# Last stage's addition of x by accumulating DMA for most tiles; sums of weights moved behind evictions or lower parts; first norm's row loaded first

## The chip, the cores and the metric

One core of a Trainium2 chip. The metric is device time in microseconds (us) of one execution of the program, as a median of several runs. The engines of the core are TensorE (PE; its weight loads are listed as PEld), VectorE (DVE), ScalarE (ACT), GpSimd (POOL) and SyncE (SP). SP issues nearly all DMAs of this kernel, each engine takes its instructions in order, and the engines wait for each other and for DMAs by semaphores.

## What is computed

One decoder layer over 1024 tokens of width 1024, in float32:

```python
def swiglu(h, w_gate, w_up, w_down):
    return (jax.nn.silu(h @ w_gate) * (h @ w_up)) @ w_down          # D_FF = 2816

x = x + 0.5 * swiglu(rms_norm(x, ffn1_norm), ffn1_w_gate, ffn1_w_up, ffn1_w_down)
h = rms_norm(x, mix_norm)
fq, fk, fv, f_logit, sq, sk, sv, g_fox, g_sb = split_columns(h @ w_in)
...                                   # forgetting attention y_fox, stick-breaking attention y_sb
merged = (jax.nn.sigmoid(g_fox) * (y_fox @ w_branch_fox) + jax.nn.sigmoid(g_sb) * (y_sb @ w_branch_sb))
x = x + merged @ w_out
x = x + 0.5 * swiglu(rms_norm(x, ffn2_norm), ffn2_w_gate, ffn2_w_up, ffn2_w_down)
x = x + jax.nn.sigmoid(rms_norm(x, ple_norm) @ w_ple_gate) * (p @ w_ple_proj)
```

## The kernel before

**Products.** Every large product is done block by block with seven products in the place of eight (Strassen's scheme in Winograd's form): a block of 256 columns of a weight is a 2x2 grid of 512 x 128 blocks, x is a 2x2 grid of 512 x 512 blocks, and seven products of sums and differences of these are added up in PSUM banks. In the code `(n, m)` is product m of weight block n: m = 1, 6, 7, 4 use one bank one after the other ("b"), 5 and 3 another ("d"), 2 a third ("a"). Each operand is split into a high part, rounded to the type TensorE multiplies at full rate (`float32r`), and a low part, the rest: ScalarE casts the high part (L105 for weights, L645 for x), VectorE subtracts for the low part (L106, L649). A product takes twelve matmuls of 512 columns: high by high, high by low, low by high, four each (L613 in `product`; L513 for the products with the down weights).

**Stages.** First FFN up and gate (22 weight blocks), first FFN down, mix projection (6 blocks of gates in this manner, the rest plainly), attention, output projection, second FFN up and gate, its down part, and the last stage, 4 blocks of `w_ple_gate`. The last chunk of a down part makes the next stage's norm and operands step by step (`up_begin`, `up_step`, `up_first`). All of these but attention are recorded in the order in which they are to stand: no scheduler moves an instruction, so the order on each engine is the order of the code.

**Steps of an up part.** `up_order` lists the products. At step s the loop takes one product, evicts what it finished (`evict`), then calls `begin(s)`, which makes the operands that only the later products need, and then `prep` for the product four steps ahead, which casts and subtracts its weight operand. The first steps of a stage (s = 0, 1, ...) are (2,1), (1,5), (2,2), (1,6), (1,7), (2,6), (2,5), (1,3), (2,7), (1,4). In `begin`, `sums(2)` (L576 to L578) makes the two sums of weight block 2 that (2,6) and (2,7) need, in a new tile and in place; `combo_s(q, 7)` casts and subtracts the four pieces of x's operand for m = 7; `last_sum` (L581) makes the weight operand of m = 2; `combo_d` (L727 and L728 in the first FFN, where x comes in rows, `rows()`; L730 elsewhere, where it comes transposed) and `combo_e` make x's operand for m = 4. Before the steps stand `combo_u` (a difference, L709 and L710, then the cast L645 on ScalarE) and `combo_s(j, 6)` (the low part L649, which waits for that cast).

**evict.** m = 1 and 6: ScalarE copies bank "b" (L770, L772; L1305 and L1307 in the mix projection, L1718 and L1720 in the last stage). The next product of that bank starts behind the copy. m = 7: a copy, and VectorE adds bank "d"; m = 3, which goes on in "d", starts behind that.

**Down parts.** `make_down` does the same with chunks of the hidden width. Step (c, i) is product i of chunk c, four banks by turns (t = 0..3), each evicted by an addition to x on VectorE (L521; L519 in the output projection). `prep` for the next step comes first, and for i = 0, 1 (behind the first chunk), 3 and 4 it ends with `wd_sums`, two subtractions of 128x1024 (L446), which are used by a `prep` one to three steps later.

**Start.** `first_entry`: ScalarE's queue issues three loads of gains (L161), then the row of the first norm (L1523, tile `PT`); SP issues x's rows and the weights. `spread` multiplies the row by ones to bring it to all partitions (L241) and copies it to SBUF (L243); `rows_mul` (L270) multiplies x's rows by it and by the rows' factors (`rt`). In the traces `in_ffn_norm_dram` stands for the first norm's row as well as for the gain of the second FFN's norm.

**Last stage.** `ple_start`: the result of a weight block is a pair of tiles of 128 x 1024, E[n][0] and E[n][1]. `fetch(n, i)` loads the matching tiles of the projection of p (`pd`, "p_proj") and of x (`xe`, "x_end"), which had been stored; `finish(n, i)` multiplies the sigmoid by the first (L1705), adds the second (L1706) and stores (L1707). The table `AT` says behind which step each is called. All these DMAs are on SP's queue, and a store waits there for VectorE. POOL has one operation in these steps, `last_sum` of block 3.

Of the kernel before, what the change touches and what calls it, by code (L numbers as in the profile page):

```python
# [18 lines left out]
P = 128  # L19
# [17 lines left out]
def tile_hybrid_decoder_layer(  # L37
# [122 lines left out]
    for i, gain in enumerate((mix_norm, ffn2_norm, ple_norm)):  # L160
        nc.scalar.dma_start(gains[:, i, :], gain[0])  # L161
# [260 lines left out]
    def make_down(wdown, hid, chunks, scale, sum_tags):  # L422
# [60 lines left out]
        def prep(c, i):  # L483
# [12 lines left out]
            if c and i < 2 or i in (3, 4):  # L496
                wd_sums(c, (1, 2, None, 3, 4)[i])
# [25 lines left out]
        return types.SimpleNamespace(wd_block=wd_block, wd_sums=wd_sums, load_hid=load_hid, operand=operand, prep=prep, product=product, chunks=chunks)  # L523
# [9 lines left out]
    def make_up(N, src, nm_, tags, first_fn, first_done=None, over=None):  # L533
# [204 lines left out]
        def begin(s):  # L738

            if s == 0:  # L740
                sums(2, nc.vector)
                for q in range(4):
                    combo_s(q, 7)
            elif s == 2:
                last_sum(1, nc.vector)
                last_sum(2, nc.vector)
            if 0 < s < 3:
                combo_d(2 * s - 2)
                combo_d(2 * s - 1)
            if 2 < s < 7:  # L750
                combo_e(s - 3)
        return types.SimpleNamespace(a=combo_a, b=combo_b, t=combo_t, l=combo_l, u=combo_u, s=combo_s, load=load, prep=prep, sums=sums, last_sum=last_sum, plain=plain, silu=silu, product=product, begin=begin, E=E, B=B, bank_of=bank_of)

    def ffn(N, wg, wu, wd, resid, hid, tags, entry, tail):
# [50 lines left out]
        with tc.manual_schedule():  # L805
# [30 lines left out]
            for s, (c, i) in enumerate(steps):  # L836
# [676 lines left out]
    def first_entry(F):  # L1513
# [20 lines left out]
        F.load(1)  # L1534
        for t in range(4):
# [60 lines left out]
        for j in range(2, 4):  # L1596
            F.u(j)
            F.s(j, 6)
# [59 lines left out]
    def second_entry(F):  # L1658
# [9 lines left out]
        for i in range(7):  # L1668
# [15 lines left out]
            for t in range(4):  # L1684
                matmuls(t)
                evict(t)
                up_step(N, Xm, xm, F, i, t)
        up_first(N, F)

    def ple_start():  # L1690
# [5 lines left out]
        def fetch(n, i, tag):  # L1696
            r = T[n, i] = [slot(tag, [P, 2, 512]) for _ in range(2)]
# [3 lines left out]
        def finish(n, i, h=slice(0, 2), cols=slice(0, 512)):  # L1701

            pt, xt = T[n, i]
            e = E[n][i]
            nc.vector.tensor_mul(e[:, h, cols], e[:, h, cols], pt[:, h, cols])  # L1705
            nc.vector.tensor_add(e[:, h, cols], e[:, h, cols], xt[:, h, cols])  # L1706
            nc.sync.dma_start(out[0, (2 * n + i) * P:(2 * n + i + 1) * P, :].rearrange("p (h n) -> p h n", h=2)[:, h, cols], e[:, h, cols])  # L1707
# [28 lines left out]
        AT = {4: [(fetch, 0, 1, "Q")], 5: [(finish, 0, 0)], 6: [(fetch, 1, 0, "KH"), (fetch, 1, 1, "T")], 7: [(finish, 0, 1)], 8: [(fetch, 2, 1, "Q")],  # L1736
# [60 lines left out]
```

## Time and profile before

| | |
|---|---|
| median of 3 runs | 2258.29 us (2256.14 to 2258.59) |
| the profiled execution | 2258.84 us |
| its span | 2257.1 us |
| instructions | 30539 |
| granted TensorE clock, mean over the span | 0.998 |
| DMA | 298.04 MB, 132 GB/s over the span |

A row of the timeline is: start (us from the span's start), duration of the run of equal instructions, engine, line, operation, output<-inputs, shape, count, and in brackets the idle time of the engine just before and what ended it. A q behind an engine's name is its queue: the issue of a DMA. A row of the table by stretches is: window, its length, then busy time and number of instructions of PE, PEld, DVE, ACT and POOL, the granted clock, the busy share of the DMA engines and GB/s. A row of waits is: who waited, for whom, us in total, times, longest. A row of DMA issues is: output<-input, count, size, median us from issue to landing. The names are those of the tiles' tags (X, H, T, Q, KH, KL, GF, RN, PT, WH, WL, RAW, Y), which many tiles share.

### The profile page before, as it was taken

The numbers are of one execution on the slowest core, as the hardware profiler recorded it, in microseconds if no ns is written. First come the engines' busy times: TensorE is split into PE (matmuls) and PEld (weight loads), VectorE is DVE, ScalarE is ACT, GpSimd is POOL, SyncE is SP. The second block draws the span as 40 slices with busy tenths as digits, with TensorE's granted clock in tenths as the row PEclk, the third lists the DMA queues.
The fourth block names the chain that finished last, engine by engine and source line by source line (L and its number), as shares of the span: only waits on it lengthen the run. The fifth ranks groups of instructions, "written<-read, shape, count | busy, mean of one in ns | idle before, by whom it ended". The sixth has DMA issues, their size and how long they took to land.

```text
span 2257.1 us, 30539 instructions
## 1 busy us (share of the span) xinstructions
PE 2218.3 (98%) x11210; PEld 1881.7 (83%) x11210; DVE 1518.7 (67%) x2371; ACT 1005.1 (45%) x1805; POOL 808.2 (36%) x782
## 2 busy tenths in 40 slices
PE   8999999999999999999999999999999999999998
PEld 6788888888888898999898888888888888888886
DVE  7755555598888334666678885889555554778797
ACT  6433333333355435555566663245333333434453
POOL 1344444210011336556566663520544353200110
PEclk9999999999999999999999999999999999999999
DMA  4232323394332434333323466741423232655325
GB/s 141 84 123 83 118 92 110 138 336 151 124 117 85 141 91 140 89 99 85 89 53 94 117 201 208 259 149 57 140 80 130 80 131 80 240 208 192 120 95 214
DMA packets 196183, 298.04 MB, mean 132 GB/s; under 512 B 28729, under 2 KB 108857, under 8 KB 196034
## 3 DMA queue, kind: packets, MB, share of 16 engines
q1 hardware_dynamic: 195600, 296.08, 39.6%
q8 instruction: 88, 1.44, 0.3%
q14 instruction: 61, 0.50, 0.1%
q10 hardware_dynamic: 434, 0.02, 0.0%
HBM read 196.14 MB, written 83.13 MB: 124 GB/s over the span
## 4 chain that ended last, share of the span: by engine, by line
PE 87%; DVE 8%; ACT 2%; issue 2%; DMA 1%; POOL 0%; SPq 0%; DVEq 0%; ACTq 0%; POOLq 0%
PE ps L613 39%; PE ps L513 20%; PE ps L885 7%; PE ps L893 5%; PE ps L1488 4%; PE ps L1226 3%; PE ps L561 3%; PE ps L1200 2%; PE ps L1142 1%; PE ps L1141 1%; PE ps L1047 1%; DVE PT L1208 1%; DVE H L106 1%; DVE RN L1104 1%; DVE GF L1104 1%
## 5 line engine op out<-in xcount | busy, mean ns | idle before, releaser
L513 PE MATMUL ps<-H,H 128*128 128x512 f32 x2184 | 498.0, 389 | 1.9 <-DVE X L521 1.2
L513 PEld LDWEIGHTS ps<-H,H 128*128 128x128 f32 x2184 | 409.2, 188 | 87.8 <-issue 3.0
L613 PE MATMUL ps<-H,WL 128*128 128x512 f32 x1164 | 276.6, 390 | 3.7 <-DVE WL L106 2.0
L613 PEld LDWEIGHTS ps<-H,WL 128*128 128x128 f32 x1164 | 218.2, 188 | 50.6 <-DVE WL L106 2.4
L187 POOL TENSOR_TENSOR PT<-PT,PT 128x512 f32<-128x512 f32 x27 | 34.9, 1294 | 405.6 <-ACT PT L184 404.7
L613 PE MATMUL ps<-H,Q 128*128 128x512 f32 x624 | 148.4, 389 | 0.0
L521 DVE SCALAR_TENSOR_TENSOR X<-ps,X 128x512 f32<-128x512 f32 x168 | 108.6, 687 | 49.3 <-PE ps L513 49.3
L613 PE MATMUL ps<-X,WL 128*128 128x512 f32 (+1 forms) x588 | 138.9, 385 | 2.1 <-ACT Y L772 1.6
L613 PEld LDWEIGHTS ps<-H,Q 128*128 128x128 f32 x624 | 117.1, 188 | 24.3
L613 PE MATMUL ps<-H,PT 128*128 128x512 f32 x540 | 131.7, 396 | 3.2 <-ACT GF L1720 3.2
L613 PEld LDWEIGHTS ps<-X,WL 128*128 128x128 f32 x588 | 108.8, 188 | 24.7 <-ACT Y L772 2.0
L613 PEld LDWEIGHTS ps<-H,PT 128*128 128x128 f32 x540 | 103.2, 192 | 25.4 <-ACT GF L1720 3.6
L139 POOL TENSOR_TENSOR WL<-RAW,WH 128x512 fp32r<-128x512 f32 (+1 forms) x84 | 97.5, 1182 | 67.2 <-ACT WH L129 43.5
L1208 DVE TENSOR_TENSOR PT<-ps,PT 128x512 fp32r<-128x512 f32 (+1 forms) x160 | 100.0, 627 | 30.0 <-ACT PT L1202 29.2
L885 PE MATMUL ps<-WH,H 128*128 128x256 f32 x768 | 116.1, 287 | 0.8 <-ACT RN L950 0.8
L893 PE MATMUL ps<-H,WH 128*128 128x512 f32 x384 | 115.1, 406 | 0.0
L1226 PE MATMUL ps<-PT,X 128*128 128x256 f32 (+1 forms) x640 | 102.4, 286 | 6.2 <-DVE PT L1208 5.2
L1202 ACT CAST PT<-ps 128x512 fp32r<-128x512 f32 (+1 forms) x160 | 87.1, 549 | 42.7 <-PE ps L1200 41.6
L1226 PEld LDWEIGHTS ps<-PT,X 128*128 128x128 f32 x640 | 90.2, 190 | 16.6 <-DVE PT L1208 10.1
L885 PEld LDWEIGHTS ps<-WH,H 128*128 128x128 f32 x768 | 101.4, 190 | 2.7 <-ACT RN L950 1.3
L414 POOL TENSOR_TENSOR PT<-GF,RN 128x512 f32<-128x512 f32 x20 | 33.7, 1685 | 188.7 <-DVE GF L795 188.7
L1154 POOL TENSOR_TENSOR T<-T,l 128x128 f32<-128x128 f32 (+3 forms) x64 | 73.2, 1147 | 71.9 <-DVE l L1153 69.7
(435 smaller groups left out, 4777.7 us busy)
## 6 DMA issues: line engine op xcount, KB each, us to landing
hidden<-PT SPq DMA_DIRECT2D x40, 512.0 KB, 3.1
WH<-in_ffn_w_gate_dram SPq DMA_DIRECT2D x38, 512.0 KB, 4.9
Q<-hidden SPq DMA_DIRECT2D x24, 512.0 KB, 6.2
hidden<-RN SPq DMA_DIRECT2D x22, 512.0 KB, 2.6
KH<-in_ffn_w_up_dram SPq DMA_DIRECT2D x20, 512.0 KB, 6.3
KL<-in_ffn_w_up_dram SPq DMA_DIRECT2D x20, 512.0 KB, 6.9
T<-in_ffn_w_down_dram SPq DMA_DIRECT2D x20, 512.0 KB, 6.4
GF<-hidden SPq DMA_DIRECT2D x14, 512.0 KB, 7.4
```

The lines of the kernel that those rows point to most:

```text
L139: ins = eng_lo.tensor_sub(lo[part], raw[part], f(hi[part]))
L513: pe(nc.tensor.matmul(groups[g][t][:], wt[:, b, k, t * P:(t + 1) * P], act[:, a, k, :], start=(fresh and n == 0), stop=(i in (6, 1, 4) and ...
L521: nc.vector.scalar_tensor_tensor(xs, groups[g][t][:], scale, xs, ALU.mult, ALU.add)
L561: pe(nc.tensor.matmul(ps[:], hl[:, a, k, :], right(rb, b, k), start=(i == 0), stop=(i == 23)))
L613: pe(nc.tensor.matmul(ps[:, cols], hl[:, a, k, :], right(B[m], b, k)[:, cols], start=(first and i == 0), stop=(final and i == 11), skip_gr ...
L885: pe(nc.tensor.matmul(ps[:, :n], hT[t // 4](a, k)[:, (t % 4) * P:(t % 4 + 1) * P], w[k // 4][b][:, k % 4, :n], start=(i == 0), stop=(i == ...
L893: pe(nc.tensor.matmul(ps[:], w[a][:, k, :], hT[half](b, k), start=(i == 0), stop=(i == 23)))
L1154: nc.gpsimd.tensor_mul(T[:, :n], T[:, :n], l[:].broadcast_to([P, n]))
L1202: high = nc.scalar.copy(pt[:, 0, :width], ps[:, :width])
L1208: ins = nc.vector.tensor_sub(pt[:, 1, :width], ps[:, :width], f(pt[:, 0, :width]))
L1226: pe(nc.tensor.matmul(o, lh, r, start=(kpair == c and i == 0), stop=(kpair == 0 and i == 3)))
L1488: pe(nc.tensor.matmul(ps[:], w[a][:, k, :], yT[g][b][:, k, half * 512:half * 512 + 512], start=(i == 0), stop=(i == 11)))
```

## The change

Four parts. (1) The loads of the gains leave ScalarE's queue and stand on SP's behind the first weights, so the first norm's row is the only load on ScalarE's queue at the start. (2) In `begin`, `sums(2)` goes from step 0, ahead of the splits for m = 7, to step 1, behind them, in all four up parts; where x comes in rows, the four `combo_d` are spread over steps 2 to 5 instead of steps 1 and 2; and in the first FFN `combo_u` and `combo_s` are called in pairs. (3) `wd_sums` leave `prep` and are called behind the second of the four evictions. (4) In the last stage `finish` no longer adds x on VectorE for six of its calls: POOL's queue issues a DMA that adds the tile of x in DRAM to the result in SBUF, the store on SP waits for that DMA, and `fetch` then loads only p's tile. The last calls (`late`) keep the addition on VectorE. `AT` is redrawn.

```diff
     gains = cp.tile([P, 3, KD], F32, name="gains")
-    for i, gain in enumerate((mix_norm, ffn2_norm, ple_norm)):
-        nc.scalar.dma_start(gains[:, i, :], gain[0])
...
-            if c and i < 2 or i in (3, 4):
-                wd_sums(c, (1, 2, None, 3, 4)[i])
...
+        def sums(c, i):
+            if c and i < 2 or i in (3, 4):
+                wd_sums(c, (1, 2, None, 3, 4)[i])
...
         def begin(s):
             if s == 0:
-                sums(2, nc.vector)
                 for q in range(4):
                     combo_s(q, 7)
+            elif s == 1:
+                sums(2, nc.vector)
             elif s == 2:
                 last_sum(1, nc.vector)
                 last_sum(2, nc.vector)
-            if 0 < s < 3:
+            if rows():
+                if 1 < s < 6:
+                    combo_d(s - 2)
+            elif 0 < s < 3:
                 combo_d(2 * s - 2)
                 combo_d(2 * s - 1)
...
                     evict_down(t)
+                    if t == 1 and s != 1 and s + 1 < len(steps):
+                        down.sums(*steps[s + 1])
...
         F.load(1)
+        for i, gain in enumerate((mix_norm, ffn2_norm, ple_norm)):
+            nc.sync.dma_start(gains[:, i, :], gain[0])
...
-        for j in range(2):
-            F.u(j)
-            F.s(j, 6)
+        for fn in (F.u, lambda j: F.s(j, 6)):
+            for j in range(2):
+                fn(j)
...
                 evict(t)
+                if t == 1 and 1 < i < 6:
+                    oproj.sums(0, i + 1)
...
-        def fetch(n, i, tag):
-            r = T[n, i] = [slot(tag, [P, 2, 512]) for _ in range(2)]
+        def fetch(n, i, *tags):
+            r = T[n, i] = [slot(tag, [P, 2, 512]) for tag in tags]
...
-        def finish(n, i, h=slice(0, 2), cols=slice(0, 512)):
-            pt, xt = T[n, i]
-            e = E[n][i]
-            nc.vector.tensor_mul(e[:, h, cols], e[:, h, cols], pt[:, h, cols])
-            nc.vector.tensor_add(e[:, h, cols], e[:, h, cols], xt[:, h, cols])
-            nc.sync.dma_start(out[0, (2 * n + i) * P:(2 * n + i + 1) * P, :].rearrange("p (h n) -> p h n", h=2)[:, h, cols], e[:, h, cols])
+        def finish(n, i, h=slice(0, 2), cols=slice(0, 512), add_in_dma=True):
+            e = E[n][i][:, h, cols]
+            nc.vector.tensor_mul(e, e, T[n, i][0][:, h, cols])
+            if add_in_dma:
+                nc.gpsimd.dma_start(e, xe[2 * n + i].rearrange("p (h n) -> p h n", h=2)[:, h, cols], accum_op=ALU.add)
+            else:
+                nc.vector.tensor_add(e, e, T[n, i][1][:, h, cols])
+            nc.sync.dma_start(out[0, (2 * n + i) * P:(2 * n + i + 1) * P, :].rearrange("p (h n) -> p h n", h=2)[:, h, cols], e)
...
-        AT = {4: [(fetch, 0, 1, "Q")], 5: [(finish, 0, 0)], 6: [(fetch, 1, 0, "KH"), (fetch, 1, 1, "T")], 7: [(finish, 0, 1)], 8: [(fetch, 2, 1, "Q")],
-              9: [(finish, 1, 0)], 10: [(finish, 1, 1), (fetch, 3, 0, "KH")], 11: [(fetch, 3, 1, "T")], 12: [(finish, 2, 1)], 13: [(fetch, 2, 0, "Q"), (finish, 3, 0, h0)],
-              16: [(finish, 3, 1, h1)], 17: [(finish, 2, 0), (finish, 3, 0, h1)]}
+        late = (slice(0, 512), False)
+        AT = {4: [(fetch, 0, 1, "Q"), (finish, 0, 0)], 6: [(finish, 0, 1), (fetch, 1, 0, "KH"), (fetch, 1, 1, "KH")], 8: [(fetch, 2, 1, "T")],
+              9: [(finish, 1, 0)], 10: [(fetch, 3, 0, "Q", "Q")], 11: [(finish, 1, 1), (fetch, 2, 0, "KH", "KH")], 12: [(fetch, 3, 1, "T", "T")],
+              13: [(finish, 2, 1)], 14: [(finish, 3, 0, h0)], 16: [(finish, 3, 1, h1, *late)], 17: [(finish, 2, 0, slice(0, 2), *late), (finish, 3, 0, h1, *late)]}
...
-                finish(3, 1, h0, cols)
+                finish(3, 1, h0, cols, False)
```

What stands where on the engines, at three places. VectorE in the first FFN, from the last `combo_u` to the steps 0 and 1, before (H is x's operand for m = 6, X that for m = 7, RAW<-WH and WH<-WH are `sums(2)`):

```order
L709 TENSOR_TENSOR KL_392<-KL_392 128x512
L710 TENSOR_TENSOR KL_392<-KL_392,GF_455 128x512
L649 TENSOR_TENSOR H_497<-KL_392,H_497 128x4x128
L106 TENSOR_TENSOR WL_541<-RAW_336,WL_541 128x512
L576 TENSOR_TENSOR RAW_560<-WH_340 128x512
L577 TENSOR_TENSOR WH_340<-WH_340,WH_341 128x4x128
L578 TENSOR_TENSOR RAW_560<-WH_340 128x512
L649 TENSOR_TENSOR X_564<-Q_294,X_564 128x4x128
L649 TENSOR_TENSOR X_564<-Q_314,X_564 128x4x128
L649 TENSOR_TENSOR X_564<-KH_357,X_564 128x4x128
L649 TENSOR_TENSOR X_564<-KL_392,X_564 128x4x128
L106 TENSOR_TENSOR WL_573<-RAW_336,WL_573 128x512
```

The same place on VectorE in the changed kernel:

```order
L710 TENSOR_TENSOR KL_392<-KL_392,GF_455 128x512
L649 TENSOR_TENSOR H_497<-KH_357,H_497 128x4x128
L649 TENSOR_TENSOR H_497<-KL_392,H_497 128x4x128
L106 TENSOR_TENSOR WL_541<-RAW_336,WL_541 128x512
L649 TENSOR_TENSOR X_560<-Q_294,X_560 128x4x128
L649 TENSOR_TENSOR X_560<-Q_314,X_560 128x4x128
L649 TENSOR_TENSOR X_560<-KH_357,X_560 128x4x128
L649 TENSOR_TENSOR X_560<-KL_392,X_560 128x4x128
L106 TENSOR_TENSOR WL_569<-RAW_336,WL_569 128x512
L576 TENSOR_TENSOR RAW_585<-WH_340 128x512
L577 TENSOR_TENSOR WH_340<-WH_340,WH_341 128x4x128
L578 TENSOR_TENSOR RAW_585<-WH_340 128x512
```

The two low parts L649 of a pair stand together behind both differences, and the three sums stand behind the four X splits and a weight's low part. The second place is ScalarE in the second FFN at steps 0 to 3, in the changed kernel; the kernel before has the same rows in the same order (with other line numbers for L774 to L778). T is x's operand for m = 7, KL what the third sum writes, L776 the copy of bank "b" behind (1,6):

```order
L645 COPY T_14525<-KH_14376 128x512
L105 COPY WL_14536<-WH_14313 128x512
L105 COPY PT_14558<-KL_14552 128x512 [waits DVE_49]
L105 COPY WL_14579<-RAW_14264 128x512 [waits PE_49,Activation_49]
L776 COPY Y_14400<-ps_14387 128x512 [waits PE_49]
```

Nothing moved there: the cast of the sum stands ahead of the copy in both, and the sum itself is now later on VectorE, which has the same order as at the first place. The third place is SP's queue in the last stage, before:

```order
L1699 DMA Q_19156<-p_proj 128x1024
L1699 DMA Q_19157<-x_end 128x1024
L1707 DMA out_dram<-GF_18851 128x1024
L1699 DMA KH_19199<-p_proj 128x1024
L1699 DMA KH_19200<-x_end 128x1024
L1699 DMA T_19203<-p_proj 128x1024
L1699 DMA T_19204<-x_end 128x1024
L1707 DMA out_dram<-RN_18852 128x1024
L1699 DMA Q_19250<-p_proj 128x1024
L1699 DMA Q_19251<-x_end 128x1024
L1707 DMA out_dram<-GF_18931 128x1024
```

SP's queue at the same place in the changed kernel:

```order
L1709 DMA Q_19154<-p_proj 128x1024
L1719 DMA out_dram<-GF_18849 128x1024
L1719 DMA out_dram<-RN_18850 128x1024
L1709 DMA KH_19198<-p_proj 128x1024
L1709 DMA KH_19200<-p_proj 128x1024
L1709 DMA T_19242<-p_proj 128x1024
L1719 DMA out_dram<-GF_18929 128x1024
L1709 DMA Q_19282<-p_proj 128x1024
L1709 DMA Q_19283<-x_end 128x1024
L1719 DMA out_dram<-RN_18930 128x1024
```

Both stores of block 0, each of which waits for an accumulating DMA, now stand ahead of the loads of p's tiles for block 1 and for E[2][1]; the store of E[1][0] stands ahead of the loads for E[3][0]. The loads of x's tiles for the first five results are gone from the queue.

More of the change, by code (lines that the diff above doesn't have):

```diff
@@ L522, in product @@
             return matmuls, evict
-        return types.SimpleNamespace(wd_block=wd_block, wd_sums=wd_sums, load_hid=load_hid, operand=operand, prep=prep, product=product, chunks=chunks)
+        def sums(c, i):
+            if c and i < 2 or i in (3, 4):
+                wd_sums(c, (1, 2, None, 3, 4)[i])
+        return types.SimpleNamespace(sums=sums, wd_block=wd_block, wd_sums=wd_sums, load_hid=load_hid, operand=operand, prep=prep, product=product, chunks=chunks)
     def up_order(nm_):
@@ L1590, in first_entry @@
         F.plain(0, 1)
-        for j in range(2):
-            F.u(j)
-            F.s(j, 6)
+        for fn in (F.u, lambda j: F.s(j, 6)):
+            for j in range(2):
+                fn(j)
         F.prep(2, 2)
         F.plain(1, 1)
-        for j in range(2, 4):
-            F.u(j)
-            F.s(j, 6)
+        for fn in (F.u, lambda j: F.s(j, 6)):
+            for j in range(2, 4):
+                fn(j)
         F.prep(1, 6)
```

## Prediction

> **What bounds the kernel now.** I read the page's first part, then the table by stretches, then the waits of TensorE, and last the timeline of each engine at the places where TensorE waits. The page's first row gives the bound:
>
> ```profile
> PE 2218.3 (98%) x11210; PEld 1881.7 (83%) x11210; DVE 1518.7 (67%) x2371; ACT 1005.1 (45%) x1805; POOL 808.2 (36%) x782
> ```
>
> TensorE is idle for 2257.1 - 2218.3 = 38.8 us, and the change takes no matmul away: idle time is all that it can win. The stretches (window, then busy time of PE, PEld, DVE, ACT, POOL) say where that lies.
>
> ```profile
> 0.00:80.00 80.00, 66.27 (x286) 50.92 (x287) 64.39 (x103) 47.10 (x93) 10.15 (x22) 0.98 0.29 99
> 2204.00:2257.00 53.00, 43.88 (x189) 35.51 (x187) 41.72 (x56) 18.52 (x33) 1.29 (x1) 0.93 0.63 228
> ```
>
> The start holds 80.00 - 66.27 = 13.7 us of it and the last stage 9.1, the tail behind the last matmul among them; most of the rest is in attention, which the change does not touch. TensorE's waits name the releasers:
>
> ```profile
> PE ps L241 <- DMA PT<-in_ffn_norm_dram: 7.7, 1, 7.7
> PE ps L613 <- ACT GF L1720: 3.8, 2, 3.2
> PE ps L613 <- ACT Y L772: 2.3, 2, 1.6
> PE ps L513 <- DVE X L521: 1.2, 2, 0.6
> PE ps L513 <- DVE X L519: 0.6, 1, 0.6
> ```
>
> A product of twelve matmuls costs 2.72 us where nothing waits: 45.98 - 43.27 in these rows.
>
> ```profile
> 43.27 2.88 PE L561 MATMUL ps<-T,WL 128*128 128x512 f32 x12
> 45.98 2.88 PE L561 MATMUL ps<-X,WL 128*128 128x512 f32 x12
> ```
>
> **First norm's row.** The three loads of gains stood ahead of the row on ScalarE's queue.
>
> ```profile
> gains<-in_mix_norm_dram ACTq DMA_DIRECT2D x1, 4.0 KB, 4.1
> gains<-in_ple_norm_dram ACTq DMA_DIRECT2D x1, 4.0 KB, 5.9
> 0.80 0.41 ACTq L161 DMA_DIRECT2D gains<-in_mix_norm_dram  x1
> 1.72 0.45 ACTq L161 DMA_DIRECT2D gains<-in_ple_norm_dram  x1
> 2.27 0.48 ACTq L1523 DMA_DIRECT2D PT<-in_ffn_norm_dram  x1
> 6.16 0.56 POOL L267 TENSOR_TENSOR rt<-ss,mhalf 128x1 f32<-128x1 f32 x1 [4.29 <-ACT ss L264]
> 7.72 3.75 PE L241 MATMUL ps<-PT,T 1*128 1x512 f32 x4 [7.72 <-DMA PT<-in_ffn_norm_dram]
> 11.51 0.69 DVE L243 COPY PT<-ps 128x512 f32<-128x512 f32 x1 [1.01 <-PE ps L241]
> 12.30 1.28 DVE L270 SCALAR_TENSOR_TENSOR PT<-X,rt,PT 128x1024 f32<-128x1024 f32 x1
> ```
>
> The third gain landed at 1.72 + 5.9 = 7.6, the first at 0.80 + 4.1 = 4.9, so one takes 1.4 of the queue; the row landed at 7.7, right behind the third. Alone it is issued at about 0.95 and lands, by the first gain's 4.1 less its own 1.4, at 3.7. All that follows (matmuls 3.75, copy 0.69, the first scaling L270) then comes 4.0 us earlier. Bounds: with the full 4.1 the gain is 2.65; with a landing at 3.0, all that L270's other input allows within some tenths (rt, ready at 6.7), it is 4.7. I take 4.0. The gains go behind the weights on SP, where nothing but three small constants follows for a while; they are needed hundreds of us later, so they cost nothing. That SP's weight loads no longer wait for a gain brings the weights sooner, which covers the shift.
>
> **First FFN's products.** From 12.3 to 76 VectorE has hardly a gap, and TensorE waits for what it makes, directly or through ScalarE.
>
> ```profile
> 54.00 0.69 DVE L649 TENSOR_TENSOR H<-Q,H 128x512 fp32r<-128x512 f32 x1 [0.69 <-ACT H L645]
> 61.23 0.69 DVE L576 TENSOR_TENSOR RAW<-WH 128x512 f32<-128x512 f32 x1
> 63.28 1.29 DVE L649 TENSOR_TENSOR X<-Q,X 128x512 fp32r<-128x512 f32 x2
> 65.16 3.02 PE L613 MATMUL ps<-X,WL 128*128 128x512 f32 x12 [1.59 <-ACT Y L772]
> 74.75 1.53 PE L613 MATMUL ps<-H,WL 128*128 128x512 f32 x4 [2.02 <-DVE WL L106]
> 76.56 3.66 PE L613 MATMUL ps<-T,WL 128*128 128x512 f32 x10 [0.27 <-DVE Y L775]
> ```
>
> With u and s in pairs the four waits of 0.69 for ScalarE's cast go: 2.7 us. The sums (61.23 to 63.28, 2.05) go behind the four splits of X, and three of four differences (1.3 each) go past the point where TensorE waited. So VectorE starts the X splits at 61.23 - 4.0 - 2.7 = 54.5, has done them and the next weight's at 57.5 and the sums at 59.6. ScalarE, in its unchanged order, must cast two results of the sums (0.5 each) before it copies the bank of product (1,6), 0.6: (1,7) starts at 61.3 instead of 65.16, although TensorE was there at 58.4. Behind it, TensorE lost 76.56 - 65.16 - 3 x 2.72 = 3.2 us; now the low part of the weight stands one difference behind the sums instead of two, and is ready near 64.7, two thirds into product (2,5) being 68.6. So (1,3) starts at 61.3 + 8.2 = 69.5: **7.1 us earlier** (4.0 of the row, 3.1 of the order). From there TensorE ran without a wait for over 300 us, so the 7.1 stay.
>
> **The same move of the sums where x comes transposed** (mix projection, second FFN, last stage). There VectorE was not behind at that place.
>
> ```profile
> 1562.21 0.69 DVE L576 TENSOR_TENSOR KL<-RAW 128x512 f32<-128x512 f32 x1
> 1562.98 1.15 ACT L645 CAST T<-KH 128x512 fp32r<-128x512 f32 x2
> 1564.54 0.62 ACT L105 CAST PT<-KL 128x512 fp32r<-128x512 f32 x1
> 1566.58 0.59 ACT L772 COPY Y<-ps 128x512 f32<-128x512 f32 x1 [0.89 <-PE ps L613]
> 1567.21 3.02 PE L613 MATMUL ps<-T,WL 128*128 128x512 f32 x12 [0.68 <-ACT Y L772]
> ```
>
> Now the sums (2.07) follow the four T splits and one weight. The splits follow ScalarE's casts, which end at 1564.13, so they end near 1564.9, the weight at 1565.5, the sums at 1567.6. ScalarE's cast of PT<-KL, begun at 1564.54 before, waits for that; then come the cast of WL and the copy L772: 1567.6 + 0.5 + 0.5 + 0.6 = 1569.3 against 1567.17. Queued behind the waiting cast is the copy that frees the bank, and TensorE waits for it: +2.1 us, with nothing behind to give it back, since TensorE alone bounds what follows. The mix projection has the same rows: **+4.2 us for the two**; the last stage's third is counted there. If the wait were covered the two would cost 0.
>
> **Sums of down weights.** Three times a pair of subtractions (2.35) stood ahead of the additions that free the banks:
>
> ```profile
> 1489.63 2.36 DVE L446 TENSOR_TENSOR RAW<-RAW,PT 128x1024 f32<-128x1024 f32 x2
> ```
>
> TensorE lost 0.62 at each (L521 twice, L519 once above). Behind two additions they are needed by a preparation in a later step, five us and more away; VectorE has slack in these stretches. **-1.9 us.** If an addition is late elsewhere, this is 0.
>
> **Last stage.** VectorE bounds it: each L1706 holds it 1.2 us.
>
> ```profile
> 2214.37 1.22 DVE L1705 TENSOR_TENSOR GF<-GF,T 128x1024 f32<-128x1024 f32 x1
> 2215.62 1.23 DVE L1706 TENSOR_TENSOR GF<-GF,T 128x1024 f32<-128x1024 f32 x1
> 2217.30 0.38 SPq L1699 DMA_DIRECT2D KH<-p_proj  x1
> 2202.93 3.02 PE L613 MATMUL ps<-H,WL 128*128 128x512 f32 x12 [0.68 <-ACT GF L1720]
> 2236.84 11.30 PE L613 MATMUL ps<-H,PT 128*128 128x512 f32 x36 [3.17 <-ACT GF L1720]
> WH<-in_w_ple_gate_dram SPq DMA_DIRECT2D x2, 512.0 KB, 3.4
> out_dram<-Y SPq DMA_DIRECT2D x2, 512.0 KB, 2.6
> KH<-p_proj SPq DMA_DIRECT2D x2, 512.0 KB, 5.5
> KH<-hidden SPq DMA_DIRECT2D x14, 512.0 KB, 9.4
> ```
>
> Six additions leave VectorE: five of 1.2 and one of 0.7, four of them ahead of the 3.17 us stall. In their place stand six DMAs on POOL's queue, which has one operation to do there. What an accumulating transfer takes is in no row; call it A, from the end of the multiplication to the landing that the store on SP waits for. Below it is bounded by the 2.6 of a store, above by 9.4, the slowest median of a 512 KB load. It reads twice what a load reads, so I add to the 3.4 of a load nearly alone the 1.3 that 512 KB take at the 400 GB/s which the DMA part reaches here: A = 4.7.
>
> The price of A is that SP issues in order. The first multiplication stands two rows earlier (ends 2214.4), the second ends at 2218.0 (four splits of 0.6 and itself). The second store waits until 2218.0 + A, and the loads KH<-p_proj, issued at 2217.30 before, go behind it: landing 0.4 + 5.5 later, at 2223.9 + A, while VectorE wants them near 2224. Behind that multiplication VectorE has 1.2 + 0.6 + 0.6 + 1.2, then the addition (0.7) for which ScalarE waits with a sigmoid, a cast and the copy (0.6 + 0.5 + 0.5): (3,7) cannot start before 2229.9 + A. TensorE itself starts (1,7) 2.1 late, at 2205.0 for 2202.93, and is there eleven products later, at 2234.9, against 2236.84. One round further, block 3's loads wait for the third store: 2225.1 + 2A, then 0.4 + 5.5, a multiplication and the addition for (3,7), 0.7 each: (3,3) cannot start before 2232.4 + 2A. Before it started at 2236.84 + 5.44 = 2242.3. By TensorE it is now 2240.3, by the loads at A = 4.7 it is 2241.8, and the end follows at the old distance: **-0.5 us**. For A of 3.9 and less it is -2.0, at 6.5 it is +3.1, at 9.4 it is +8.9; it turns at 4.95.
>
> [...] No row before has a DMA from POOL.
>
> **Sum.** -7.1 + 4.2 - 1.9 - 0.5 = -5.3 us. The profiled execution took 2258.84 (span 2257.1), 0.55 over the median of the three runs, 2258.29. So 2253.5 by the one and 2253.0 by the other; I say **2253.2**.
>
> **Rivals.**
> 1. The accumulation is quick (A under 4). For it: POOL idles, and stores of that size land in 2.6. The last stage then wins 2.0, TensorE being the bound: 2251.8. Chance 0.2.
> 2. It is slow, 6.5 to 9: SP's order then gives back what was won, +3 to +8 on -4.8, 2257 to 2262, no change that can be told for most of it. For it: loads here take 5.5 to 6.6 in company. Chance 0.15.
> 3. Slower than before: the same chain, A above 9.6, since 2A - 9.9 must exceed 4.8 + 4.5. Place: SP's stores in the last stage, with both rounds in a row. For it: the 9.4 of some loads, and an untried path; against it: the stage's DMA queues have gaps. 2264 at A = 10. Chance 0.08.
> 4. The sums moved in the transposed cases cost nothing, because a cast could go ahead: 2249.0. Against it: the cast reads what the third sum writes, and ScalarE's order is unchanged. Chance 0.07.
> 5. The row was not what held the start, so the change does not do that part: if x's tiles or the weights hold L270, 4.0 less, 2257.2. Against it: L270 starts 0.1 behind the copy of the row, and its other input, rt, was ready at 6.7. Chance 0.06.
>
> The forecast keeps 0.44. A measurement of this kernel can tell 0.2% or 4.5 us, a bound of 2253.8: the forecast lies just beyond it, so I give 0.29 of its 0.44 to faster, with rivals 1 and 4: 0.56. Slower 0.09, the rest 0.35. Range: 2248.5, rival 4 with a quick start, to 2260.0, the middle of rival 2; about a tenth on each side is left out. The forecast's own range is 2251 to 2256.
>
> **What would show it.** The matmul that spreads the row starts near 3.7 and L270 near 8.3; TensorE reaches (1,3) near 69.5, with a wait of about 3 us before (1,7) and none after. Near 700 and 1560 TensorE's wait before (1,7) is 2.8 instead of 0.68. The waits on L521 and L519 are gone. In the last stage the wait before (3,7) is under 1 us, and the new one stands before (3,3), released by VectorE and behind it a load; SP's stores start A behind the multiplications. I am wrong if A is over 6 or if the transposed cases show no longer wait.

## The result

The changed kernel took **2265.31 us** (median of 6 runs, 2264.37 to 2266.34) against 2258.45 for the kernel before on the same chip (6 runs, 2256.14 to 2259.04): a ratio of 1.0032, 95% interval 1.0019 to 1.0045. It is 6.9 us slower; the forecast was 2253.2, 5.3 faster. The profiled execution took 2264.37 (span 2262.6).

The page's first row, then TensorE's waits (engine, tile and line <- releaser: us in total, times, longest):

```profile
PE 2217.6 (98%) x11210; PEld 1884.4 (83%) x11210; DVE 1511.6 (67%) x2365; ACT 1005.6 (44%) x1805; POOL 817.4 (36%) x788
```

```profile
PE ps L613 <- ACT RN L1771: 9.2, 1, 9.2
PE ps L613 <- ACT Y L776: 6.1, 2, 3.2
...
PE ps L239 <- DMA PT<-in_ffn_norm_dram: 3.8, 1, 3.8
PE ps L613 <- ACT GF L1313: 2.9, 1, 2.9
PE ps L613 <- ACT GF L1732: 2.9, 1, 2.9
```

TensorE's busy time is on balance what it was, 2217.6 for 2218.3, so the loss shows as idle time. The wait for the row has halved (7.7 to 3.8), the three waits on the old L519 and L521 are gone; the waits for L1313, L776 and L1732 are the three moved sums, and on top stands one wait of 9.2 us that the forecast did not have. The stretches say the same (window, length, busy time of PE, PEld, DVE, ACT, POOL, granted clock, DMA share, GB/s):

```profile
0.00:80.00 80.00, 71.33 (x321) 56.35 (x322) 69.99 (x111) 49.31 (x97) 11.10 (x22) 1.00 0.32 109
2204.00:2263.00 59.00, 44.42 (x192) 36.62 (x192) 34.33 (x49) 18.88 (x33) 6.76 (x7) 0.88 0.75 218
```

The start gained 5 us of TensorE time (66.27 before). In the last stage VectorE is relieved by 7 us (41.72 to 34.33) and the stage still became longer.

Pairing the same matmul in the two traces shows where the lead arose and went (starts on TensorE; minus is ahead of before):

| place | before | after | lead |
|---|---|---|---|
| row spread over the partitions | 7.72 | 3.80 | -3.92 |
| (1,3) of the first FFN | 76.56 | 69.82 | -6.74 |
| end of the first FFN, L194 (L196 before) | 644.43 | 635.67 | -8.76 |
| mix projection, last third of (1,7) | 707.18 | 702.03 | -5.15 |
| second FFN, at (1,7) | 1567.21 | 1565.61 | -1.60 |
| second FFN, one product behind | 1570.07 | 1569.88 | -0.19 |
| end of the second FFN, L194 (L196 before) | 2142.14 | 2141.07 | -1.07 |
| last stage, (1,7) | 2202.93 | 2204.05 | +1.12 |
| last stage, one product behind | 2205.79 | 2208.25 | +2.46 |
| last stage, next to last half product | 2247.97 | 2244.67 | -3.30 |
| last stage, last half product | 2250.04 | 2255.50 | +5.46 |

Two places eat most of the gain: each moved sum (8.76 ahead becomes 5.15 at the first; at the second the lead was still 3.85 ahead of the product in which it falls to 0.19), and the last 15 us of the program. Another 1.3 us of lead (5.15 to 3.85) goes between the mix projection and the second FFN, and its cause is not shown.

**The end.** VectorE's timeline in the last stage, the multiplications (L1714) of tiles (0,0), (1,1) and (2,1) first, then the end (start, length, line, operation, what the idle time before it waited for):

```profile
2212.18 1.22 DVE L1714 TENSOR_TENSOR GF<-GF,T 128x1024 f32<-128x1024 f32 x1
...
2230.24 1.22 DVE L1714 TENSOR_TENSOR RN<-RN,KH 128x1024 f32<-128x1024 f32 x1
...
2234.88 1.22 DVE L1714 TENSOR_TENSOR Y<-Y,T 128x1024 f32<-128x1024 f32 x1
...
2241.66 0.68 DVE L1742 TENSOR_TENSOR Y<-Y,ps 128x512 f32<-128x512 f32 x1
2251.96 0.69 DVE L1714 TENSOR_TENSOR RN<-RN,T 128x512 f32<-128x512 f32 x1 [9.62 <-DMA T<-p_proj]
2253.22 0.69 DVE L1718 TENSOR_TENSOR RN<-RN,T 128x512 f32<-128x512 f32 x1 [0.57 <-DMA T<-x_end]
2253.83 0.68 DVE L1742 TENSOR_TENSOR GF<-GF,ps 128x512 f32<-128x512 f32 x1
```

SP's queue and POOL's, and then TensorE:

```profile
2219.55 0.36 SPq L1719 DMA_DIRECT2D out_dram<-GF  x1
...
2234.79 0.34 SPq L1719 DMA_DIRECT2D out_dram<-GF  x1
...
2237.60 0.34 SPq L1719 DMA_DIRECT2D out_dram<-RN  x1
2238.05 0.75 SPq L1709 DMA_DIRECT2D KH<-p_proj  x1
2238.89 0.43 SPq L1709 DMA_DIRECT2D KH<-x_end  x1
2239.36 0.64 SPq L1709 DMA_DIRECT2D T<-p_proj  x1
2240.09 0.58 SPq L1709 DMA_DIRECT2D T<-x_end  x1
2246.20 0.34 SPq L1719 DMA_DIRECT2D out_dram<-Y  x1
```

```profile
2232.04 0.90 POOL L1716 DMA_DIRECT2D RN<-x_end  x1 [1.73 <-DVE RN L1714]
2236.67 0.88 POOL L1716 DMA_DIRECT2D Y<-x_end  x1 [3.73 <-issue]
```

```profile
2241.79 3.04 PE L613 MATMUL ps<-H,PT 128*128 128x512 f32 x12 [0.72 <-DVE RN L1735]
2244.67 1.59 PE L613 MATMUL ps<-X,WL 128*128 128x256 f32 x12
2255.50 2.93 PE L613 MATMUL ps<-X,WL 128*128 128x256 f32 x12 [9.24 <-ACT RN L1771]
```

Read backwards: TensorE's last product waits for a bank that ScalarE (L1771) frees; ScalarE stands behind the sigmoid of GF; that needs VectorE's addition L1742; and L1742 stands on VectorE behind tile (3,1)'s multiplication, which waits for T<-p_proj. Nothing but a store needs that multiplication. VectorE's order made it everyone's. The load was issued at 2239.36, since on SP it stands behind the store of RN (2237.60), which waited 6.1 us for its accumulation (the multiplication ended at 2231.46). And it took 12.5 us to land. Before, the same load was issued at 2235.74, and the two loads of this tile landed 5.7 and 6.6 us after their issue (least, median, most of the two):

```profile
2235.74 0.44 SPq L1699 DMA_DIRECT2D T<-p_proj  x1
DMA to landing us min/median/max: 5.7/6.2/6.6
```

From 2204 to the end the queues of the changed kernel moved (packets, MB, share of 16 engines' time):

```profile
q1 hardware_dynamic: 3552, 9.96, 46.2%
q0 software_dynamic: 864, 2.88, 28.8%
```

The accumulations, on POOL's queue (q0), carry 2.88 MB and use 28.8% of the DMA engines, ten points a megabyte; the loads and stores (q1) use under five.

### The profile page after: what moved, and what is told of

It reads as the page before. It is cut to its first block, busy times and chain, and to the rows that moved or that the text cites. A ratio compares the mean times of both kernels' runs of the same rounds, so it can differ in the third digit from the quotient of the medians.

```text
span 2262.6 us, 30509 instructions
## 1 busy us (share of the span) xinstructions
PE 2217.6 (98%) x11210; PEld 1884.4 (83%) x11210; DVE 1511.6 (67%) x2365; ACT 1005.6 (44%) x1805; POOL 817.4 (36%) x788
## 3 DMA queue, kind: packets, MB, share of 16 engines
q0 software_dynamic: 864, 2.88, 0.8%
```

## The experiments

Each was run in alternation with the kernel before on its chip. The difference is the median less the median of before beside it; the ratio is of this kernel to before.

| run | what it is | median us | before | difference | ratio, 95% interval |
|---|---|---|---|---|---|
| change | | 2265.31 | 2258.45 | +6.9 | 1.0019 to 1.0045 |
| 1 | change, last stage as before | 2258.16 | 2258.49 | -0.3 | 0.9988 to 1.0006 |
| 2 | change, sums first where x is transposed | 2257.99 | 2258.49 | -0.5 | 0.9987 to 1.0005 |
| 3 | both | 2249.88 | 2258.49 | -8.6 | 0.9947 to 0.9972 |
| 4 | change, stores behind the loads | 2260.15 | 2258.49 | +1.7 | 0.9998 to 1.0016 |
| 5 | change, plain loads from POOL | 2262.18 | 2258.39 | +3.8 | 1.0005 to 1.0023 |
| 6 | run 3, block 0 accumulated | 2251.02 | 2258.39 | -7.4 | 0.9953 to 0.9978 |
| 7 | run 3, row late again | 2253.88 | 2258.39 | -4.5 | 0.9972 to 0.9990 |
| 8 | run 3, down weights' sums early again | 2251.96 | 2258.39 | -6.4 | 0.9960 to 0.9982 |
| 9 | run 3, block 1 accumulated | 2248.68 | 2258.18 | -9.5 | 0.9947 to 0.9972 |
| 10 | runs 4 and 5 together | 2256.04 | 2258.18 | -2.1 | 0.9981 to 0.9998 |
| 11 | run 3, first FFN's old order | 2251.95 | 2258.18 | -6.2 | 0.9962 to 0.9983 |
| 12 | run 9, sums first everywhere | 2243.83 | 2257.74 | **-13.9** | 0.9922 to 0.9949 |

### Runs 1 to 3: which part lost it

Run 1 puts the old fetch, finish and table back:

```
-  e = ...; multiply; nc.gpsimd.dma_start(e, x_end, accum_op=ALU.add); store
+  multiply; nc.vector.tensor_add(e, e, xt); store
-  AT = {4: [(fetch, 0, 1, "Q"), (finish, 0, 0)], ...}
+  AT = {4: [(fetch, 0, 1, "Q")], 5: [(finish, 0, 0)], ...}
```

> The changed kernel with the last stage's multiplications, additions, loads and stores as before (no accumulating DMA); the three other parts stay. Theory A (the loss is made in the last stage, by loads that stand on SP behind stores that wait for accumulations, and by slow accumulations): the changed kernel reached the last stage 1.1 us ahead of before (2141.07 against 2142.14), and the old stall of 3.17 us before (3,7) absorbs what the moved sums cost inside the stage, so 2258.45 - 1.1 = about 2257.4 (2256.5 to 2259), with no wait of 9 us before TensorE's last product. Rival B (the loss is the moved sums, and the last stage would have been as late with additions on VectorE): 2263 or more. Rival C (forecast's own prices, +2.1 for each moved sum, -0.5 for the accumulations): 2254.

Run 2 puts the sums back into step 0, except in the first FFN:

```
-  if s == 0: combos
-  elif s == 1: sums(2, nc.vector)
+  if s == (1 if rows() else 0): sums(2, nc.vector)
+  if s == 0: combos
```

> The changed kernel with the four sums of a block back in the first step where x comes transposed (mix projection, second FFN, last stage) and late only in the first FFN; accumulations stay. Theory A, with the price read off the two traces (each moved sum costs 3.5 us: 2.2 of longer wait and 1.3 of matmuls at a granted clock of 0.55 to 0.66 right behind it): TensorE enters the last stage 7.1 us earlier than the changed kernel, the tail's chain of loads follows, so 2265.3 - 7.1 = 2258.2, and down to 2254.8 if the third sum's 3.5 come off as well. Rival C (2.1 each, no clock): 2265.3 - 4.2 = 2261.1, with the third 2259. The wait of about 9 us before the last product stays in every theory.

Run 3 makes both edits.

> Both edits together: what is left of the change is the row first, the first FFN's order and the down weights' sums. Theory A: TensorE is 1.1 + 7.1 = 8.2 us ahead of before at the entry of the last stage and keeps it: 2258.45 - 8.2 = 2250.2 (2249.5 to 2251.5), faster than both kernels. Rival C (sums at 2.1 each): 2258.45 - 1.1 - 4.2 = 2253.1. A rival by which attention gives the gain back: 2255 or more.

Measured: -0.3, -0.5 and -8.6. Theory A holds in all three; B does not, and the forecast's own prices (rival C) fail in runs 1 and 3 (in run 2, with the third sum counted, they are 1 us off, within the interval). Taking back the accumulations is worth 7.2 us with the late sums (change against run 1) and 8.1 without (run 2 against run 3). Taking back the late sums is worth 7.4 (change against run 2) and 8.3 (run 1 against run 3). The two losses add up, and what remains gains 8.6.

Why the sums cost more than the 4.2 forecast for the two is seen behind the wait. The mix projection, first its matmuls, then the same time in stretches with the granted clock (third number from the end), all of the changed kernel:

```profile
698.75 2.08 PE L613 MATMUL ps<-T,WL 128*128 128x512 f32 x4 [2.87 <-ACT GF L1313]
700.63 1.57 PE L613 MATMUL ps<-Y,WL 128*128 128x512 f32 x4
702.03 1.09 PE L613 MATMUL ps<-T,WL 128*128 128x512 f32 x4
```

```profile
698.75:702.00 3.25, 3.25 (x8) 2.63 (x9) 3.25 (x7) 0.11 (x1) 0.00 (x0) 0.55 0.21 36
702.00:705.00 3.00, 3.00 (x14) 2.44 (x13) 2.38 (x4) 2.12 (x4) 0.00 (x0) 1.00 0.40 139
```

The wait itself was forecast at 2.8 and is 2.87. Then TensorE runs at a granted clock of 0.55 for 3.3 us. The second FFN has the same pair: a wait of 2.92, then 1569.88 - 1565.61 = 4.27 for a product that took 1570.07 - 1567.21 = 2.86 before. So one moved sum costs 2.2 of added wait and 1.4 of slow clock, 3.6, as the table of leads has it.

### Runs 4, 5 and 10: what is slow in the last stage

Run 4 keeps the accumulations and issues a store only after the loads of the next blocks; it also calls the loads of tile (3,0) one step earlier. In part:

```
-  def finish(n, i): mul; accumulate; store
+  def finish(n, i): mul; accumulate
+  def put(n, i): store
-  11: [(finish, 1, 1), (fetch, 2, 0)], 12: [(fetch, 3, 1)]
+  11: [(finish, 1, 1), (fetch, 2, 0)], 12: [(fetch, 3, 1), (put, 1, 0), (put, 1, 1)]
```

> The changed kernel, accumulations and all, but SP issues the last stage's loads ahead of the stores that wait for an accumulation (block 3's and block 2's loads of p_proj and x_end no longer stand behind the stores of blocks 0 and 1). Theory A1 (SP's order makes the loss): the loads of tile (3,1) are issued near 2232 instead of 2239.4 and land before 2246, the wait of 9.2 us before the last product is under 1.5, and the time is 2265.3 - 8 = about 2257 (2256 to 2259). Theory A2 (the accumulations' own use of the DMA engines makes it: 28.8 % of engine time for 2.88 MB against 46.2 % for 9.96 MB of all the rest): the same bytes must pass in the same time whatever the order, the loads of (3,1) land near 2250 all the same, the wait before the last product stays above 6 us, and the time stays above 2262.

Measured: +1.7, so 5.2 us better than the change: between A1 and A2. The loads of (3,1) are now issued at 2234.17 and 2234.88, and still land late:

```profile
2247.31 0.69 DVE L1718 TENSOR_TENSOR RN<-RN,T 128x512 f32<-128x512 f32 x1 [2.37 <-DMA T<-p_proj]
2250.20 0.69 DVE L1722 TENSOR_TENSOR RN<-RN,T 128x512 f32<-128x512 f32 x1 [2.20 <-DMA T<-x_end]
```

```profile
2252.48 2.66 PE L613 MATMUL ps<-X,WL 128*128 128x256 f32 x12 [4.11 <-ACT RN L1776]
```

T<-x_end took 15.2 us from issue to landing, although it was issued 1.4 us earlier than before (2236.28). So SP's order is one cause; that the traffic of the accumulations is the other is what runs 5 and 10 test.

Run 5 leaves SP's order as the change has it and makes the six transfers plain loads, so that these tiles lose the product and hold x alone.

```
-  nc.gpsimd.dma_start(e, x_end[...], accum_op=ALU.add)
+  nc.gpsimd.dma_start(e, x_end[...])
```

> The changed kernel with the six transfers on POOL's queue as plain loads that overwrite the tile, where they accumulated into it: so the output of those tiles lacks the product with p_proj and the gate, and only x_end is left in them. Same queue, same issues, same waits, same bytes on the wire in one direction. Theory A2a (adding in flight costs the DMA engines a second pass): the POOL queue's share of engine time in the last stage falls from 28.8 % to about half, 12 to 16, a transfer that met no company takes 1.5 us less than the 6.0 of an accumulation, the wait before the last product falls from 9.2 us to 4 or less, and the time from 2265.3 to 2258 to 2261. Theory A2b (it is the queue of POOL that is slow, whatever the transfer does): share and time stay within 1.5 us of the changed kernel's.

Measured: +3.8, 3.1 better than the change: outside A2b's 1.5, and in A2a's direction but less than its 4 to 7; the share and the wait, below, miss A2a's figures too. POOL's queue in the last stage of run 5, and two of its issues (engine, count, KB each, median us to landing), against the same two of the change:

```profile
q0 software_dynamic: 800, 2.88, 17.0%
```

```profile
GF<-x_end POOLq DMA_DIRECT2D x2, 512.0 KB, 3.8
RN<-x_end POOLq DMA_DIRECT2D x2, 512.0 KB, 4.4
```

```profile
GF<-x_end POOLq DMA_DIRECT2D x2, 512.0 KB, 5.4
RN<-x_end POOLq DMA_DIRECT2D x2, 512.0 KB, 5.4
```

The same bytes on the same queue take 17.0% of the engines where accumulating took 28.8 (of a stretch of 56 us for 59), and land 1.0 to 1.6 us sooner. So adding in flight cost the DMA engines nearly twice here (28.8% of 59 us against 17.0% of 56: 1.8 times); the queue of POOL as such cost little (5.9 points a megabyte in run 5, where the loads and stores of that run take 48.9% for 9.96 MB, 4.9 points). TensorE still waits 6.7 us at the end, with SP's order unchanged.

Run 10 has both edits.

> The changed kernel with both edits of the last stage: the stores behind the loads, and the six transfers on POOL's queue as plain loads (so the product with p_proj and the gate is missing from those tiles). If SP's order (-5.2 in the fourth run) and the second pass of adding (-3.1 in the fifth) are two causes that add up, 2265.3 - 8.3 = 2257.0 (2256 to 2258.5), with a wait before the last product under 2 us. If both act on one thing, the time at which the loads of tile (3,1) have passed, the second gives less once the first is gone: 2258.5 to 2260.

Measured: -2.1, 9.0 better than the change, where 5.2 + 3.1 = 8.3 had been expected, and no long wait is left before the last product (0.47). With run 4's order on SP, the two loads of tile (3,1) now landed 7.6 and 8.6 us after their issue, where they took 13.1 and 15.2 beside the accumulations. The two causes add up and cover the loss in the last stage.

### Runs 7, 8 and 11: the parts that gained

Each is run 3 with one part undone.

```
run 7:  the three loads of gains back on ScalarE's queue, ahead of the row
run 8:  wd_sums(c, ...) back in prep(c, i); no sums(...) behind the second eviction
run 11: for j: F.u(j); F.s(j, 6)  (no pairs);  combo_d twice in steps 1 and 2;  sums first
```

> The kernel of the third run with the three loads of gains ahead of the first norm's row on ScalarE's queue again. By the forecast's term 4.0 us are lost: 2249.9 + 4.0 = 2253.9 (2252.5 to 2255). Rival (the row did not hold the start): 2250. Rival (a part comes back in the first FFN's stalls, where the two traces differ by 3.7 just ahead of (1,3)): 2251 to 2252.5.

> The kernel of the third run with the sums of the down weights back inside the preparation, ahead of the additions that free the banks. By the forecast's term 3 x 0.62 = 1.9 us are lost: 2251.8. By the two traces' starts of the same matmuls 0.9 at each of the second FFN's two places and nothing at the other: 1.75, so 2251.6. Rival (it is covered elsewhere): 2250.

> The kernel of the third run with the first FFN's sums, differences and pairs (u, s) in the old order; the first norm's row stays early. By the forecast's term 3.1 us are lost: 2249.9 + 3.1 = 2253.0. By the starts of the same matmuls in the traces of before and of the change (8.0 ahead behind that place, 3.9 ahead at the row) 4.0: 2253.9. Rival (the gain of the row and that of the order are one and the same, VectorE's chain being as long from wherever it starts): 2250.

Measured against run 3's -8.6: the row is worth 4.1 us (4.0 forecast), the down weights' sums 2.2 (1.9), the first FFN's order 2.4 (3.1; of the 4.0 read from the traces 1.6 did not come back). The sum, 8.7, is run 3's gain; the single prices come from medians that scatter by about 1 us, and the intervals of runs 8 and 11 overlap run 3's, so these two are not clear of noise by the times alone. The traces agree with them: in run 8 TensorE waits 1.8 us in three places for the additions that free the banks, in run 3 in none; (1,3) starts at 72.70 in run 11, at 69.83 in run 3.

### Runs 6 and 9: can an accumulation pay

Run 6 accumulates block 0's two tiles only, stores behind block 1's loads:

```
-  4: [(fetch, 0, 1, "Q")], 5: [(finish, 0, 0)], 6: [fetches of block 1], 7: [(finish, 0, 1)]
+  4: [(fetch, 0, 1, "Q"), (finish, 0, 0, accumulate)], 6: [(finish, 0, 1, accumulate), fetches of block 1], 8: [(put, 0, 0), (fetch, 2, 1), (put, 0, 1)]
```

> The kernel of the third run (sums first where x is transposed, last stage as before), with the two tiles of block 0 alone accumulated by DMA and their stores behind block 1's loads. Theory A: these two are issued in the part of the stage whose DMA engines still have gaps, and nothing that is needed soon stands behind their stores; VectorE has 2.4 us less ahead of the addition that (3,7) waits for, so the stall of 3.2 us there falls under 1 and with it the slow clock behind it: 2249.9 - 2.5 to - 5.5, 2244.4 to 2247.4. Theory D (any accumulation delays the loads of the crowded stretch, since the engines' total time sets the end): 2250 to 2253.

Measured: -7.4, no gain on run 3: a miss for theory A, by a wait that it had not seen. ScalarE's timeline:

```profile
2223.73 0.59 ACT L1734 COPY GF<-ps 128x512 f32<-128x512 f32 x1 [6.44 <-DMA out_dram<-GF]
```

Block 3 evicts into the slot that block 0 leaves, so the copy waits for block 0's store to land, and that store was late by the 9.1 us that its accumulation took beside block 1's four loads. The stall before (3,7) was gone, and one of 3.25 us stood two products earlier.

Run 9 accumulates block 1's two tiles, whose slots nobody takes, and stores them behind all loads:

```
-  9: [(finish, 1, 0)], 10: [(finish, 1, 1), (fetch, 3, 0)]
+  9: [(finish, 1, 0, accumulate)], 10: [(finish, 1, 1, accumulate), (fetch, 3, 0)], 13: [(fetch, 2, 0), (put, 1, 0), (put, 1, 1), (finish, 3, 0, h0)]
```

> The kernel of the third run with the two tiles of block 1 alone accumulated by DMA, and their stores issued behind all loads of the stage. No later tile takes the place of these two, so nothing but the stores waits for the accumulations. Theory A (what an accumulation costs is paid only by what waits for it): VectorE has 2.45 us less right ahead of the addition that (3,7) waits for, the stall of 3.2 us there falls to 0.7 or less and the slow clock behind it goes (9.94 us for 36 matmuls becomes 8.3): 2249.9 - 2 to - 4 = 2246 to 2248. Theory D (the accumulations, about twice a plain transfer for the DMA engines, delay block 3's and block 2's loads, which land when the last tiles want them): the wait comes back before the last product, 2250 to 2253.

The stage does as theory A says; run 9's row at (3,7), and run 3's:

```profile
2227.59 8.83 PE L613 MATMUL ps<-H,PT 128*128 128x512 f32 x36 [0.66 <-ACT GF L1736]
```

```profile
2227.82 9.94 PE L613 MATMUL ps<-H,PT 128*128 128x512 f32 x36 [3.19 <-ACT GF L1730]
```

The accumulations took 9.8 and 11.2 us to land and nobody waited. From the entry of the stage to the last products TensorE gains 5.0 us on before, in run 3 1.4. But the time, -9.5 beside -8.6, is not clearly better than run 3's: the interval of the ratio is the same. The profiled execution of run 9 had lost 1.4 us in the first FFN, where a wait of 3.1 before (1,7) was followed by a slow product (4.46 us), as run 3's was not (3.03).

### Run 12: the sums first everywhere

That wait is in all the kernels with late sums in the first FFN. Run 12 is run 9 with the sums first there too.

```
-  if s == (1 if rows() else 0): sums(2, nc.vector)
   if s == 0:
+      sums(2, nc.vector)
       combos
```

> The kernel of the ninth run with the four sums first in the first FFN too, so that of the change there only the pairs (u, s) and one difference at a time are left. Theory E (the late sums cost there what they cost elsewhere, a wait of 2 to 3 us before (1,7), and the gain of the first FFN comes from the pairs and the differences alone): the wait of 3.1 us before (1,7) falls to 1 or less, the slow clock that follows it in some executions goes, and 2248.7 falls by 2 to 4, to 2245 to 2247. Theory F (VectorE is behind in this stretch, the only one where it is: sums that come first make the splits of x late, as the forecast assumed): a wait of 2 us or more appears at the products behind, (1,3) starts no earlier than in the ninth run, and the time is 2248 to 2251.

Measured: 2243.83, 13.9 us faster than before and 4.4 better than run 9: theory E, a little past its 2 to 4. The first FFN of run 12:

```profile
59.24 3.02 PE L613 MATMUL ps<-X,WL 128*128 128x512 f32 x12 [0.68 <-ACT Y L775]
62.09 2.88 PE L613 MATMUL ps<-H,PT 128*128 128x512 f32 x12
64.81 2.88 PE L613 MATMUL ps<-H,WL 128*128 128x512 f32 x12
67.53 2.88 PE L613 MATMUL ps<-T,WL 128*128 128x512 f32 x12
```

(1,3) starts at 67.53, against 76.56 before and 69.82 in the change. This is the best version: the row first, the pairs (u, s), one difference at a time, the down weights' sums behind two evictions, the sums of a block where they always were, and accumulations for block 1 alone.

## Why the prediction was wrong

**First norm's row: right.** TensorE's first matmul at 3.80 (forecast near 3.7), the first scaling at 8.37 (near 8.3); run 7 prices it at 4.1 for 4.0.

**First FFN's products: right in place, half right in cause.** The forecast had (1,7) at 61.3 behind a wait of about 3 us and (1,3) at 69.5; the trace has

```profile
61.50 3.04 PE L613 MATMUL ps<-X,WL 128*128 128x512 f32 x12 [3.16 <-ACT Y L776]
64.38 2.88 PE L613 MATMUL ps<-H,PT 128*128 128x512 f32 x12
67.10 2.88 PE L613 MATMUL ps<-H,WL 128*128 128x512 f32 x12
69.82 2.88 PE L613 MATMUL ps<-T,WL 128*128 128x512 f32 x12
```

Run 11 measures 2.4 for the forecast's 3.1. But the forecast took the late sums for part of the gain; run 12 shows that they are a loss here as elsewhere, and that the pairs and the differences carry it.

**Sums of down weights: right.** 1.9 forecast, 2.2 by run 8; the two agree within the scatter.

**The moved sums where x comes transposed: right mechanism, mis-sized.** The chain was as described, a cast that waits for the third sum with the copy that frees the bank queued behind it, and the waits of 2.87 and 2.92 were forecast at 2.8. The term of +4.2 for two left out what TensorE does behind such a wait: in the traces the two cost 3.6 and 3.7, and by runs 1 to 3 the times give 7.4 to 8.3 for all three. That is a quarter to a third of the error of 12 us; the rest is the last stage. The rows for it stood in the forecast's own fences: before, 36 matmuls behind the stall of 3.17 us took 11.30 us, where three products without a wait take 8.2.

**The last stage: the step that failed.** The term was -0.5; by runs 1 to 3 it is +7.2 to +8.1. Its last clause, that "the end follows at the old distance", is where it broke. Up to (3,3) the chain held in its order: (3,7) without a wait, and (3,3) behind VectorE and a load. The forecast followed SP's order one tile short. Tile (3,1)'s loads stand behind the fourth store, and they met the accumulations on the DMA engines. The time A of an accumulation was mis-sized too: 4.7 forecast; for the first four it is 5.7 to 6.2 (the first multiplication ended at 2213.40, its store was issued at 2219.55), and 10.1 beside the six loads (2236.10 to 2246.20). The 4.7 rests on an accumulation's reading twice what a load reads; no run shows what it reads, only that it took the DMA engines 1.8 times as long as the plain load of run 5. That (3,3) started at 2241.79 for the forecast's 2241.8 is luck: the two accumulations on its path took 5.9 and 5.7, which the forecast's formula turns into 2244, but the second multiplication ended 1.1 us sooner than forecast and the loads of p's tiles landed 4.6 and 5.3 us after their issue for the 5.5 assumed. Had the clause been true, an A of 6 would have cost some 2 us by the forecast's formula. The forecast's own sign of being wrong, A over 6, is there. The nearest rival was the third, SP's stores in order with both rounds in a row: the right place, but its point of decision (A above 9.6) came from the same short chain. Part of the price is no matter of order at all (run 4: 4.1 us of wait left); no rival had that.

The terms as measured, 4.1 + 2.4 + 2.2 gained and 7.4 plus 7.2 lost, give 5.9 slower, and with the larger values of the last two 7.7; the measurement is 6.9.

## What to carry over

Here the addition that moved from a busy engine to a DMA moved onto three in-order queues at once: the one that issued it (POOL's), the one whose store had to wait for it (SP's, 6.1 us for RN's tile), and that of every engine that needed a later load behind that store (VectorE's, 9.62 us idle). Follow each to the last tile, not to the first place where the sum looks even, and give a transfer to such a queue only where nobody takes its slot and no load stands behind its store (runs 6 and 9). A wait of TensorE of about 3 us is to be priced with a slow stretch behind it: in the rows here that cost between nothing and as much again (36 matmuls in 11.30 us for 8.3 behind 3.17 us).

## What the runs showed of the hardware

**The granted clock behind a wait of 3 us went either way.** The same wait at the same place, before (1,7) of the second FFN, in the change, then in run 5:

```profile
1565.61 4.43 PE L613 MATMUL ps<-T,WL 128*128 128x512 f32 x12 [2.92 <-ACT Y L776]
```

```profile
1567.85 3.06 PE L613 MATMUL ps<-T,WL 128*128 128x512 f32 x12 [2.92 <-ACT Y L776]
```

The granted clock is 0.54 behind the one and 1.00 behind the other; what decides is not shown. In the first FFN the wait of 3.1 to 3.2 us was followed by a product of 3.03 to 3.06 us in the change and in runs 2, 3 and 8, and of 4.34 to 5.49 in runs 1, 4, 5, 6, 7, 9 and 10. Behind the wait of 0.68 us that the kernel before has in the second FFN, the product took 3.02 us, at a granted clock of 1.00; behind its wait of 2.02 us shortly ahead of (1,3) in the first FFN, the granted clock was 0.70 over the next 5.8 us.

**An accumulating DMA into SBUF** of 512 KB landed 5.4 us (median) after its issue in the change, a plain one from the same queue 3.8 to 4.4 in run 5 and 6.1 to 6.3 in run 10; the six accumulations used the engines 28.8% of 59 us, the six plain ones 17.0% of 56 in run 5 and 13.7% of 56 in run 10. With other loads about, accumulations of that size took 9.1 and 9.5 us in run 6 and 9.8 and 11.2 in run 9; the plain transfer that stands beside the six loads took 9.0 (run 5), and the accumulation in its place 9.5 (the change).

**The types on TensorE.** Twelve `float32r` matmuls of 512 columns took 2.72 us in the first FFN of the change (67.10 to 69.82), 0.23 each. Its two float32 matmuls of 512 columns that spread the row (L239, four rows) took 3.75 us behind the first wait, 1.9 each, and the four bf16 ones next to them (L253) 1.89, 0.47 each; no row has `float32r` beside another type at the same place.
